# Stick-breaking layer: memory query projections ahead of the first pair, and the memory attention's steps dealt out from the first unit on

## The chip, the cores and the metric

One NeuronCore of one Trainium2 chip runs the whole program. The metric is device time in microseconds (us), the median of three timed executions. A profiled execution is one more, with its own time and a span from its first to its last instruction. Engines: PE is TensorE (its weight loads, PEld, overlap), DVE is VectorE, ACT is ScalarE, POOL is GpSimd, SP is SyncE.

## The reference

A trunk of two layers over 512 tokens of width 1024, all in float32. Layer 0 mixes with a gated delta rule, layer 1 with stick-breaking attention; both also attend over 256 memory tokens. The part that the change touches is layer 1's mixer:

```python
q, k, v = ...                          # 12 heads of 64
for blk in range(4):                   # blocks of 128 queries
    z = einsum('bthd,bshd->bhts', q[blk], k[:t1]) * 0.125
    log_1m_beta = where(before, log_sigmoid(-z), 0)
    tail = cumsum(log_1m_beta, reversed) - log_1m_beta
    a = where(before, exp(log_sigmoid(z) + tail), 0)
    out[blk] = a @ v
mem_q = proj[..., 3 * W:]              # 4 heads of 64
cross = softmax(mem_q @ mem_k.T * 0.125) @ mem_v
y = concat([mix, cross]) @ w_out       # then norm, residual and the MLP
```

## The kernel before

Every matrix product is done in three passes of a split format: each float32 operand is cut by ACT into a rounded high part (L199, `whi`) and by DVE into the rest (`split_lo`, L176, `wlo`), and PE adds hi*hi, hi*lo and lo*hi into one PSUM bank (`mm3`, L207 to L213; the matmuls are on L212). The activations live transposed, as `h_hi` and `h_lo`. PSUM has eight banks: four of the tag `acc` and four of the tag `g` (L89).

**Order of the work.** The Python text gives each instruction a place, and that is its rank. When the program is made, each engine's queue is filled by taking the ready instruction of the best rank, and an instruction whose tile has no free slot yet is passed by until one comes free. So an instruction of later rank runs early when its inputs and a slot are there, and on the chip each engine then runs its queue in order.

**The stick-breaking stage** (L1261 to L1301). `sb_values` (L1032) makes the six value tiles `vv`, one for each pair of heads, in a ring of six slots with the tag `v`. `sb_qk` (L1062) projects one pair: two pieces of 24 matmuls, each handed out in slices of 9, 9 and 6 (`fm_slices`, L220), each holding one `acc` bank from its first matmul until DVE has read it (L1071 to L1077). `stick_breaking` (L1148) then runs 36 units, three for each head, the two heads of a pair one step apart. Step n does three things:

- `sb_scores` of unit n: matmuls into a `g` bank, three ACT functions (L1100 to L1102), then DVE's max-and-add (L1103), a cast and a split.
- `sb_weights` of unit n-2: the cumulative sums as matmuls (L1122), ACT's exponential, a DVE cast (L1128) and a POOL subtraction (L1129) into two-slot tiles.
- `sb_av` of unit n-4: weights times values (L1141). A head's three units add up in one `acc` bank, which is held from the first of them until ACT and DVE have copied it (L1145, L1146). A pair's value tile is let go after its second head, which for pair p is step 6p+10.

After each step the loop of L1289 asks the next pair's projection for a slice, and asks the generator `fill` (L1284) for as many steps as `FILLN` (L1316) has for this n: one row of six numbers for each pair of heads.

`fill` hands out the memory work. `mem_queries` (L1279) is two projections like the ones above, six steps of 9, 9 and 6 matmuls, with the results put away by L664 (ACT) and L665 (DVE). `mem_attention` (L669) is 20 steps for four heads and two halves of the tokens:

- eight *scores* steps (4 matmuls L691; DVE max L694; two ACT exponentials L698; DVE reciprocal L700 and two multiplications L702), with two slots for the result `p`;
- eight *turn* steps (4 transposes L711 into an `acc` bank; then two ACT copies L714 and two DVE splits into the tiles `pT`), two `pT` tiles for each head. These tiles have the tag `v`: they take slots of the ring of value tiles;
- four *values* steps (4 matmuls L722, an ACT copy L725, a DVE addition L726), in an `acc` bank.

The order is scores 1, scores 2, turn 1, scores 3, turn 2, scores 4, turn 3, values 1, and so on to turn 8 and values 4.

In this kernel the 6 + 20 steps go out at every second n: the six query steps at n = 1 to 11, the first nine steps of the attention at n = 13 to 29, and its last eleven at n = 30 to 36.

**After the stage.** `out_early` (L787) multiplies the first three of eight row blocks of `w_out`, 36 matmuls into all four `acc` banks, and `out_proj` (L801) goes on; neither's first blocks need the memory result or the last pair.

Of the kernel before, what the change touches and what calls it, by code (L numbers as in the profile page):

```python
# [62 lines left out]
def drain(gen):  # L63
    for _ in gen:
        pass
# [1104 lines left out]
def build(ctx, tc, a, out):  # L1170
# [27 lines left out]
    with tc.tile_pool(name="gdn", bufs=1, reuse_waits="tile") as gp:  # L1198
# [11 lines left out]
        def alloc(name):  # L1210
            if name == "p":
                return gp.tile([P, 2, NMEM], F32, name=name, tag="t2", bufs=3)
            if name == "o":
                return gp.tile([P, S], F32, name=name, tag="t2", bufs=3)
            t = gp.tile([P, 2, S], F32R, name=name, tag="kq" if name == "pTh" else "UI", bufs=3)
            return t[:, 0], t[:, 1]

        def fill(gi):
            if gi < 2:
                yield from k.qkv_group(gi + 1, hi, lo, gp, parts[gi + 1],  # L1220
                                       k.gates((2 * gi, 2 * gi + 1), hi, lo, mixT))
            else:
                yield from k.gates((4, 5), hi, lo, mixT)
                for c in range(2):
                    qm.append([gp.tile([P, S], F32R, name="qm", tag=x, bufs=2) for x in ("kT", "vT")])
                    yield from k.mem_q(win[4 * H + 1 + c], hi, lo, qm[c])
                yield from k.mem_attention(0, qm, alloc, mixT)
                yield from k.out_early(0, mixT, st)
        st = {}
        for gi in range(3):  # L1230
            weave(k.gdn_group(gi, parts[gi], gp, mixT), fill(gi), SCALE[gi], lambda n: n % 3 or k.tick(1))
# [29 lines left out]
    with tc.tile_pool(name="sb", bufs=1, reuse_waits="tile") as sp:  # L1261
        tc.keep_in_program_order(nc.scalar.preload_act_table_set("natural_log_exp_and_others"))
        vv = k.sb_values(hi, lo, sp, later[0])
        mixT = k.act.tile([P, KC, S], F32, name="mixT", bufs=1)
        qks = [{} for _ in range(H)]
        drain(k.sb_qk(0, hi, lo, sp, qks[0]))
        qm = []

        def alloc(name):
            if name == "p":  # L1270
                return sp.tile([P, 2, NMEM], F32, name=name, bufs=2)
            if name == "o":
                return sp.tile([P, S], F32, name="sb_o", bufs=1)
            if name == "w":
                return sp.tile([P, 512], F32, name=name, tag="p", bufs=2)
            t = sp.tile([P, 2, S], F32R, name="pT", tag="v", bufs=H)
            return t[:, 0], t[:, 1]

        def mem_queries():  # L1279
            for c in range(2):  # L1280
                qm.append([sp.tile([P, S], F32R, name="qm", bufs=4) for x in "hl"])
                yield from k.mem_q(a["w_b_qk"][2 * H + c], hi, lo, qm[c])

        def fill():  # L1284
            yield from mem_queries()
            yield from k.mem_attention(1, qm, alloc, mixT)
        extra = fill()
        proj = None
        for n in k.stick_breaking(qks, vv, sp, mixT):  # L1289
            pair, u = divmod(n + LAG, 6)  # L1290
            if (u == 0 or n == 0) and pair + 1 < H:
                proj = k.sb_qk(pair + 1, hi, lo, sp, qks[pair + 1])
            if u < 5:
                next(proj, None)
            for _ in range(FILLN[min(n // 6, H - 1)][n % 6]):
                next(extra, None)
            if u == 5:
                drain(proj)
        drain(extra)
        st = {}  # L1300
        drain(k.out_early(1, mixT, st))  # L1301
# [11 lines left out]


GROUPS = (16, 12)
FILLN = ((0, 1, 0, 1, 0, 1),) * 5 + ((2, 1, 2, 1, 2, 1),)  # L1316
SCALE = (1.0, 1.0, 1.0)
YS = (2.0, 2.0, 1.5, 0.5, 2.0, 1.8, 1.2, 1.2, 1.2, 1.2, 0.8, 0.9, 0.8, 3.0)
_F = np.ascontiguousarray
# [49 lines left out]
```

## Time and profile before

| | us |
|---|---|
| median of 3 runs (1320.36 to 1321.84) | 1320.38 |
| the profiled execution | 1318.39 |
| its span | 1316.7 |
| PE busy in the span | 1275.9 (97%) |
| DVE busy | 861.8 (65%) |
| ACT busy | 717.5 (54%) |
| POOL busy | 163.9 (12%) |

The profiled execution has 1.69 us around its span and is 1.99 us under the median. Busy time of PE is counted from modelled ends of pipelined matmuls, so a PE shown as full need not be at its peak; the other engines' busy time is a fair measure. The granted clock of PE is 0.993 over the span.

### The profile page before, as it was taken

To read this page: it belongs to the slowest core of one execution; us is meant where nothing else is said; L and a number is where in the kernel's file an instruction comes from. 1 tells how busy PE (TensorE), PEld (TensorE's weight loads), DVE (VectorE), ACT (ScalarE), POOL (GpSimd) and SP (SyncE) were. 2 spreads that over 40 slices of the span, in tenths; PEclk is the share of its full clock that TensorE was granted. 3 is DMA by queue.
4 is the path that set the end of the run, shared out by engine and by line. 5 is a ranking of instruction groups with operands and counts; after the bars stand their busy time and mean duration, and the time that the engine had idled before them with its cause. 6 is when DMAs were issued, how large, how long until landed. Compare 5 with 4: busy or idle time off the path is not lost.

```text
span 1316.7 us, 18097 instructions
## 1 busy us (share of the span) xinstructions
PE 1275.9 (97%) x6620; PEld 1070.0 (81%) x6620; DVE 861.8 (65%) x1588; ACT 717.5 (54%) x1378; POOL 163.9 (12%) x196
## 2 busy tenths in 40 slices
PE   7999999998999999999999999998999999999997
PEld 7788878887788888878888988786788888878886
DVE  7677695877663264555788678999573255455776
ACT  8654435446455454444565567878455344454561
POOL 2511313010021000000000013223130000000000
PEclk9999999999999999999999999999999999999999
DMA  7551654415689878644454426222679944544441
GB/s 242 192 166 58 161 130 117 123 51 143 210 245 266 233 190 243 195 145 143 148 186 139 157 75 150 76 64 64 208 255 256 257 127 144 148 141 150 152 144 64
DMA packets 82153, 209.39 MB, mean 159 GB/s; under 512 B 6720, under 2 KB 11840, under 8 KB 81616
## 3 DMA queue, kind: packets, MB, share of 16 engines
q1 hardware_dynamic: 62192, 164.12, 37.7%
q0 software_dynamic: 19296, 43.06, 16.4%
q8 instruction: 52, 0.85, 0.3%
q10 hardware_dynamic: 576, 1.05, 0.2%
q14 instruction: 37, 0.30, 0.1%
HBM read 199.29 MB, written 67.63 MB: 203 GB/s over the span
## 4 chain that ended last, share of the span: by engine, by line
PE 80%; DVE 10%; ACT 6%; issue 2%; DMA 1%; POOL 0%; SPq 0%; DVEq 0%; POOLq 0%; ACTq 0%
PE ps_acc L212 45%; PE ps_g L955 21%; PE ps_g L212 4%; PE ps_g L526 1%; PE ps_g L1122 1%; DVE wlo L176 1%; PE ps_g L389 1%; PE ps_g L518 1%; ACT whi L199 1%; PE ps_g L488 1%; ACT scrap L281 1%; DVE cv L360 1%; PE ps_g L295 1%; DVE sb_e L1103 1%; PE ps_acc L1141 1%
## 5 line engine op out<-in xcount | busy, mean ns | idle before, releaser
L212 PE MATMUL ps_acc<-h_hi,whi 128*128 128x512 f32 (+1 forms) x888 | 338.1, 381 | 0.0
L212 PE MATMUL ps_acc<-h_hi,wlo 128*128 128x512 f32 (+1 forms) x888 | 337.5, 380 | 0.0
L212 PE MATMUL ps_acc<-h_lo,whi 128*128 128x512 f32 (+1 forms) x888 | 335.1, 377 | 0.0
L176 DVE TENSOR_TENSOR wlo<-raw,whi 128x1024 fp32r<-128x1024 f32 x134 | 169.2, 1264 | 141.3 <-ACT whi L199 133.9
L955 PE MATMUL ps_g<-whi,sh 128*128 128x512 f32 x784 | 261.1, 395 | 0.0
L199 ACT ACTIVATE whi<-raw 128x1024 fp32r<-128x1024 f32 x134 | 141.8, 1059 | 203.0 <-PE ps_g L955 94.1
L176 DVE TENSOR_TENSOR wlo<-xc,whi 128x1024 fp32r<-128x1024 f32 x89 | 108.8, 1224 | 151.2 <-ACT whi L199 149.0
L212 PEld LDWEIGHTS ps_acc<-h_hi,wlo 128*128 128x128 f32 x888 | 167.5, 189 | 34.0 <-DVE wlo L176 3.9
L212 PEld LDWEIGHTS ps_acc<-h_hi,whi 128*128 128x128 f32 x888 | 167.8, 189 | 28.8 <-ACT whi L199 1.6
L212 PEld LDWEIGHTS ps_acc<-h_lo,whi 128*128 128x128 f32 x888 | 167.9, 189 | 28.4
L955 PEld LDWEIGHTS ps_g<-whi,sh 128*128 128x128 f32 x784 | 147.6, 188 | 34.5
L199 ACT ACTIVATE whi<-xc 128x1024 fp32r<-128x1024 f32 x89 | 94.3, 1060 | 137.1 <-PE ps_g L955 92.5
L955 PE MATMUL ps_g<-wlo,sh 128*128 128x512 f32 x392 | 154.8, 395 | 0.0
L955 PEld LDWEIGHTS ps_g<-wlo,sh 128*128 128x128 f32 x392 | 73.9, 189 | 17.2
L882 POOL DMA_DIRECT2D sum<-w_down x56 | 51.5, 1332 | 181.8 <-DMA sum<-w_down 104.4
L176 DVE TENSOR_TENSOR sh<-ua,sh 128x512 fp32r<-128x512 f32 x98 | 66.7, 685 | 4.7 <-ACT sh L936 4.7
L1129 POOL TENSOR_TENSOR sb_al<-sb_a,sb_ah 128x384 fp32r<-128x384 f32 (+1 forms) x36 | 41.2, 1144 | 154.8 <-DVE sb_ah L1128 133.1
L936 ACT ACTIVATE sh<-ua 128x512 fp32r<-128x512 f32 x98 | 59.9, 618 | 0.3
L212 PE MATMUL ps_acc<-ua 128*128 128x512 f32 x224 | 57.3, 391 | 0.0
L978 POOL DMA_DIRECT2D ua<-park x4 | 2.3, 574 | 388.6 <-DVE sh L176 381.2
L212 PEld LDWEIGHTS ps_acc<-ua 128*128 128x128 f32 x224 | 42.0, 188 | 8.9
L212 PE MATMUL ps_acc<-whi,h_hi 128*128 128x256 f32 (+1 forms) x144 | 44.5, 326 | 0.0
(352 smaller groups left out, 2148.2 us busy)
## 6 DMA issues: line engine op xcount, KB each, us to landing
sum<-w_down POOLq DMA_DIRECT2D x56, 512.0 KB, 9.9
xc<-w_up SPq DMA_DIRECT2D x38, 512.0 KB, 3.9
xc<-w_down SPq DMA_DIRECT2D x30, 512.0 KB, 3.9
xc<-sum SPq DMA_DIRECT2D x29, 512.0 KB, 4.0
sum<-w_down SPq DMA_DIRECT2D x28, 512.0 KB, 6.5
sum<-sum SPq DMA_DIRECT2D x28, 512.0 KB, 5.4
raw<-w_in_a SPq DMA_DIRECT2D x27, 512.0 KB, 3.8
raw<-sum SPq DMA_DIRECT2D x27, 512.0 KB, 3.7
```

The lines of the kernel that those rows point to most:

```text
L176: self.nc.vector.tensor_tensor(out=lo, in0=src, in1=f(hi), op=ALU.subtract)
L199: self.nc.scalar.activation(out=hi, in_=raw, func=AF.Copy)
L212: self.nc.tensor.matmul(out, lhsT=l, rhs=r, start=start and k == 0 and i == 0, stop=stop and k == n - 1 and i == 2)
L281: nc.scalar.activation(out=self.scrap(m), in_=x[:, j * m:(j + 1) * m], func=AF.Square, accum_out=ssq[:, j:j + 1])
L295: op = nc.tensor.transpose(b[:, j, i * P:(i + 1) * P], xs[i][:, (kc + j) * P:(kc + j + 1) * P], self.ident)
L360: nc.vector.scalar_tensor_tensor(out=acc[:, j:], in0=b[:, :S - j], scalar=w[:, 3 - j:4 - j], in1=acc[:, j:], op0=ALU.mult, op1=ALU.add)
L389: self.nc.tensor.transpose(tp[:, t], src(t), self.ident)
L488: nc.tensor.matmul(sb[:, j], lhsT=self.sel[:, s4 + j], rhs=ud, start=True, stop=True)
L882: self.tc.keep_in_program_order(nc.gpsimd.dma_start(out=dst, in_=src, accum_op=ALU.add))
L936: nc.scalar.activation(out=s[:, 0], in_=src, func=AF.Copy)
L955: nc.tensor.matmul(y[t], lhsT=l, rhs=r, start=new and d == 0 and z == 0 and m == 0, stop=d == nd - 1 and z == 1 and m == 2, skip_group_che ...
L1129: nc.gpsimd.tensor_tensor(out=u["al"], in0=a, in1=f(u["ah"]), op=ALU.subtract)
```

## The change

The two query projections leave `fill` and are drained before it is made, that is after the first pair's projection and before unit 0. `fill` keeps the 20 steps of the attention alone, and `FILLN` is dealt anew: one step at n = 1, 3, ..., 23, two in each row's first half from n = 24 on, so that the 20th goes out at n = 35. No instruction is added or taken away.

```diff
         def fill():
-            yield from mem_queries()
             yield from k.mem_attention(1, qm, alloc, mixT)
+        drain(mem_queries())
         extra = fill()
...
-FILLN = ((0, 1, 0, 1, 0, 1),) * 5 + ((2, 1, 2, 1, 2, 1),)
+FILLN = ((0, 1, 0, 1, 0, 1),) * 4 + ((1, 1, 0, 1, 0, 1),) * 2
```

In the new numbering scores 1 to 4 stand at n = 1, 3, 7 and 11, turns 1 to 3 at n = 5, 9 and 13, values 1 at n = 15, and turns 7 and 8 and values 3 and 4 in the last six steps.

## Rows read from the trace of the kernel before

**Rows 1.** The page, busy time of each engine over the span.
```profile
PE 1275.9 (97%) x6620; PEld 1070.0 (81%) x6620; DVE 861.8 (65%) x1588; ACT 717.5 (54%) x1378; POOL 163.9 (12%) x196
```

**Rows 2.** Windows: stretch, length; busy (count) of PE, PEld, DVE, ACT, POOL; clock, DMA.
```profile
745.00:763.00 18.00, 18.00 (x110) 16.02 (x108) 7.31 (x12) 6.72 (x13) 0.00 (x0) 1.00 0.53 186
765.40:818.30 52.90, 52.90 (x288) 44.50 (x286) 43.56 (x70) 38.33 (x69) 13.02 (x13) 1.00 0.44 104
818.30:870.10 51.80, 48.89 (x282) 41.52 (x280) 48.54 (x84) 41.00 (x86) 13.38 (x13) 1.00 0.29 81
870.10:895.00 24.90, 23.63 (x135) 19.72 (x135) 23.90 (x42) 20.81 (x43) 8.29 (x8) 1.00 0.38 81
895.00:926.00 31.00, 26.58 (x144) 19.45 (x143) 29.70 (x66) 24.08 (x61) 12.55 (x11) 1.00 0.19 63
```

**Rows 3.** The chain that ended last: start, us, what.
```profile
765.95 4.09 PE ps_acc L212 x18
```

**Rows 4.** Groups by line, 763 to 926 us: count, busy us, mean ns, idle before.
```profile
L176 DVE TENSOR_TENSOR wlo<-raw,whi 128x1024 fp32r<-128x1024 f32 x13 | 15.8, 1216 | 3.0 <-ACT whi L199 2.9
L702 DVE TENSOR_SCALAR p<-p,sm 128x256 f32<-128x256 f32 x16 | 8.6, 576 | 0.1
L176 DVE TENSOR_TENSOR pT<-ps_acc,pT 128x256 fp32r<-128x256 f32 x16 | 6.6, 416 | 0.8 <-ACT pT L714 0.7
L694 DVE TENSOR_REDUCE nmx<-ps_acc 128x2 f32<-128x512 f32 x8 | 5.5, 684 | 0.1
L665 DVE SCALAR_TENSOR_TENSOR qm<-ps_acc,qm 64x512 fp32r<-64x512 f32 x4 | 2.8, 690 | 0.1
L726 DVE TENSOR_TENSOR mixT<-ps_acc,sb_o 64x512 f32<-64x512 f32 x4 | 2.7, 685 | 0.1
```

**Rows 5.** Windows of the maximum L694 alone: stretch, length, DVE busy (count), clock, DMA.
```profile
818.30:870.10 51.80, 2.04 (x3) 1.00 0.29 81
...
895.00:926.00 31.00, 2.75 (x4) 1.00 0.19 63
```

**Rows 6.** Windows of the tile pT alone; columns as in rows 2, without POOL.
```profile
818.30:870.10 51.80, 0.00 (x0) 0.00 (x0) 1.67 (x4) 1.54 (x4) 1.00 0.29 81
...
895.00:926.00 31.00, 3.88 (x12) 2.02 (x12) 4.13 (x10) 3.83 (x10) 1.00 0.19 63
```

**Rows 7.** Timeline: start, us, instruction; units 0 and 35, a query result, the last mixT.
```profile
762.60 0.22 PE L1092 MATMUL ps_g<-sbqh,sbkk 128*128 128x128 f32 x1
765.39 0.49 ACT L1100 ACTIVATE sb_e<-ps_g 128x384 f32<-128x384 f32 x1
821.12 0.59 ACT L664 ACTIVATE qm<-ps_acc 64x512 fp32r<-64x512 f32 x1 [0.66 <-DVE qm L665]
912.72 0.60 ACT L1100 ACTIVATE sb_e<-ps_g 128x512 f32<-128x512 f32 x1
927.13 0.69 DVE L1146 TENSOR_TENSOR mixT<-ps_acc,sb_o 64x512 f32<-64x512 f32 x1 [0.72 <-ACT sb_o L1145]
```

**Rows 8.** Timeline of who holds `acc` banks around turn 3 (876 to 904 us).
```profile
876.18 0.60 PE L711 MATMUL ps_acc<-ident,p 128*128 128x128 f32 x4
878.90 0.39 PE L212 MATMUL ps_acc<-h_hi,whi 128*128 128x512 f32 x1
882.38 0.30 PE L1141 MATMUL ps_acc<-sb_ah,v 128*128 128x128 f32 x1
886.40 0.40 PE L1141 MATMUL ps_acc<-sb_al,v 128*128 128x512 f32 x1
888.78 0.42 DVE L176 TENSOR_TENSOR pT<-ps_acc,pT 128x256 fp32r<-128x256 f32 x1
889.26 1.19 PE L722 MATMUL ps_acc<-pT,mv 128*128 128x512 f32 x4 [0.68 <-DVE pT L176]
894.42 0.69 DVE L176 TENSOR_TENSOR sbkk<-ps_acc,sbkk 64x512 fp32r<-64x512 f32 x1
903.35 0.66 DVE L1146 TENSOR_TENSOR mixT<-ps_acc,sb_o 64x512 f32<-64x512 f32 x1
```

## The prediction

> **What bounds the kernel now.** I read the page first, then windows over the stage that the change touches, then the chain of waits inside it, and last the groups of instructions and the timeline. The page says that PE is busy for 97% of the span and DVE for 65% [rows 1]. Over 1317 us that hides stages with other limits, so the windows come next. They are cut where the scores of units 0, 12, 24 and 30 reach ACT: 765.4, 818.3, 870.1 and 895 us, with 926 as the end of the stage.
>
> The reader is to see in them that the limit changes inside the stage [rows 2]. In the first twelve units PE is full (52.90 of 52.90 us) and DVE has 9.3 us left over (43.56 of 52.90). In the next twelve DVE is busy for 48.54 of 51.80 and PE, even by its generous count, for 48.89. From 895 us on DVE is busy for 29.70 of 31.00 and PE for 26.58. So the stage begins with PE as its bound and ends with DVE as its bound, and the chain of waits agrees: it starts out as runs of projection matmuls, 18 of them in 4.09 us [rows 3], and later goes through ACT and DVE. The counts tell why. The first stretch holds both query projections, which are much PE work and little DVE work. The last one holds four of the eight scores steps (the maximum, x4) [rows 5], five of the eight turns (two splits each, x10) and three of the four values steps (x12 matmuls) [rows 6].
>
> Ahead of the stage, from 745 to 763 us, PE is full too, with DVE busy for only 7.31 of 18 us [rows 2]. That is the neighbourhood into which the queries move.
>
> **The change part by part.** No instruction comes or goes. So I price the places: how much of DVE's and of PE's work each stretch holds afterwards, and how long the stretch must then last. For a stretch that DVE bounds I divide its DVE work by the share at which DVE ran in the three later stretches, (48.54 + 23.90 + 29.70) / (51.80 + 24.90 + 31.00) = 0.948 [rows 2]. The work of a step is the sum of its DVE durations [rows 4]: a scores step 0.684 + 2 x 0.576 = 1.84 us, a turn 2 x 0.416 = 0.83, a values step 0.69. A query projection has a weight split of 1.22 and two results of 0.69.
>
> *The queries ahead of unit 0.* 48 matmuls at 4.09 / 18 = 0.228 us [rows 3] are 10.9 us in which PE is full and no unit's scores are issued. Unit 0's first matmul moves from 762.60 [rows 7] to 773.5. Its ACT step does not move as far: today it stands at 765.39 [rows 7], 2.8 us behind that matmul, since ACT is still copying the second projection of the first pair. Afterwards that copying is long done, and I put it some 0.7 us behind the matmul, at 774.2, which is 8.8 late. The ends are 8.8 and 10.9; I take +9.0, near the first, since nothing else stands before it on ACT. Two more issues move with the steps: the two weight loads on SP's queue, which then stand ahead of pair 1's, and the two background copies that each finished projection lets out. DMA was at 0.53 there and 0.44 behind it [rows 2], so I price them at nothing; were a weight late, PE would wait in the open, at most for one piece (5.5 us).
>
> *Units 0 to 11.* PE loses 10.9 of its 52.9 us, so the bound is now DVE: 43.56, less two weight splits and two of the four results (the other two are late, at 821.12 [rows 7]), which is 3.81, plus four scores steps, 7.36. That is 47.1, or 49.7 at 0.948, against 52.9: -3.2.
>
> Only scores steps come in, not turns, and this is the point of the change that the ring decides. A head's two `pT` tiles take slots of the value tiles. Those of pairs 0 and 1 are let go at n = 10 and n = 16, so turns 1 and 2, which are dealt out at n = 5 and 9, can't be finished before n = 16, about where turn 1 stands today (n = 17).
>
> *Units 12 to 23.* Out go the two late query results (1.38), three scores and two turns (7.18). In come five turns, one values step and two scores steps (8.52). 48.54 becomes 48.5, or 51.2 us: -0.6.
>
> *Units 24 to 29.* One of each (3.36, what the neighbours leave of 8, 8 and 4) becomes two scores, one turn and one values step (5.20). 25.7 / 0.948 = 27.2 against 24.9: +2.3.
>
> *The last stretch.* Four scores, five turns and three values steps (13.6) become two turns and two values steps (3.0). If DVE stays the bound, 10.5 / 0.948 = 11.1 us go. But the last unit's own chain runs through every engine: it starts at 912.72 and its sum into `mixT` ends at 927.82 [rows 7]. If those 15.1 us stay as they are, only the 17.7 us before them shrink, by 10.5 / 29.7 of their length, 6.3. I take -9.0, the middle, because a chain with DVE free waits less but can't vanish. What is late next is that chain, and behind it `out_early`, which is PE work with no need of the last pair and can fill PE's free time once two of four banks are free.
>
> *Banks held by turns that can't finish.* The trace shows one such turn: turn 3's transposes at 876.18 take a bank, the slot for its low part comes free with the last matmul of pair 3 (886.40), DVE lets the bank go at 889.2, and PE then starts the values step that had stood still for 0.68 us [rows 8]. Afterwards turns 1 and 2 both stand so, from about n = 9 to 16. A head holds a bank for 21.6 us (882.38 to 904.01) and a projection for 16.2 (878.90 to 895.11) [rows 8]. A pair needs 2 x 21.6 + 2 x 16.2 = 75.6 bank-us, and on two banks this takes 37.8 us where twelve units in 51.8 give a pair 25.9. If nothing gives way, 7 units of hold cost 7/6 x 11.9 = 13.9 us. If a projection is squeezed to its 24 x 0.228 = 5.5 us of PE time, 54.2 on two banks is 27.1, and the cost is 1.4. I take +1.4, since it agrees with two holds at the 0.68 that one costs today, and since a unit's weights may lag two steps behind its scores.
>
> The sum is 9.0 - 3.2 - 0.6 + 2.3 - 9.0 + 1.4 = -0.1 us on a span of 1316.7. The profiled execution was 1318.39, 1.99 under the median of the runs shown, and I carry the difference over to that median: 1320.3 us. The change moves work from a full place to another nearly full place, and the start that it delays costs what the end gives back.
>
> A rule weighs against the change here. The rows show the first stretch with both kinds of work woven together, at full PE and 0.82 of DVE [rows 2]. The Trainium skill, in "Perfetto Trace Analysis", section "Optimization Strategy", says that where the most-contended engine changes over time, interleaving the regimes may help. Dealing out the attention follows it; draining the queries in one block undoes it. By the rule the block costs its whole 10.9 us instead of 9.0, and the sum would be +1.8.
>
> **The rivals.**
>
> *Bank famine, slower.* Between n = 9 and 16 the heads and projections get two of four `acc` banks; a head that waits for one keeps its two-slot weight tiles, the next units' weights stop behind them, and with four score tiles in flight DVE runs out of work. For it speaks that turn 3 shows the mechanism on one bank [rows 8]; against it that projections have been paced by rank, not by need. It decides as soon as turn 2's transposes get their bank before the second pair's first head gets its own. At the middle of its two ends, 7.5 in place of 1.4: +6.0, 1326.4 us.
>
> *DVE fills up, faster.* With scores steps at hand from the first unit, DVE may run at its full share and the end may give all 11.1: 47.1 - 52.9 + 48.5 - 51.8 + 25.7 - 24.9 - 11.1 + 8.8 = -10.6 without bank waits. Nothing in the trace runs at 1.0 over such a length, so I take somewhat over half: -6, 1314.4 us. For it speaks that DVE had 9.3 us free in the first stretch, against it that 0.948 held in all three later ones [rows 2].
>
> *The attention does not move.* The order is made by readiness, and the ring lets no turn go earlier. If the scores steps, too, wait for banks behind earlier ranks, only the queries move: the first stretch is then 39.8 of DVE (41.9) against 42.0 of PE, -10.9, the second -1.5, the start +9.0. That is -3.4, 1317.0 us.
>
> **How the numbers follow.** About 2.6 us (0.2%) is what a measurement of this kernel tells from no change. The forecast, -4 to +3 around -0.1, has 0.42, of which 0.09 lie past the bound on the fast side and 0.06 on the slow. Bank famine has 0.25, all slower; the full DVE 0.21, all faster; the attention that does not move 0.12, of which 0.07 are past the bound. So faster is 0.09 + 0.21 + 0.07 = 0.37, slower 0.06 + 0.25 = 0.31, no change 0.32. The forecast's own range is 1316.4 to 1323.3. The range to hold the time 8 times in 10 takes in both outer rivals' middles, 1313 to 1327, and leaves out the far half of bank famine's prices and of the full DVE's.
>
> **What would show it.** Right: unit 0's ACT step at about 774; units 12 and 30 about 6 and 8 us later than now; DVE near 0.95 from the first unit on; the last stretch shorter by 6 to 11. Turn 1's low part stands at or behind n = 16. Wrong: an idle DVE of several us between units 9 and 16 with a head's first matmul waiting for a bank (famine); a share of 0.97 or more throughout, and `out_early` done inside the last unit's chain (faster); scores steps no earlier in units than now.

## The result: slower by 0.9%

| | before | after |
|---|---|---|
| median, runs side by side | 1320.37 us (1319.66 to 1321.84, 4 runs) | 1331.28 us (1330.38 to 1331.81, 4 runs) |
| span of the profiled execution | 1316.7 us | 1328.7 us |
| granted clock over that span | 0.993 | 0.989 |

The ratio is 1.0093, with a 95% interval of 1.0071 to 1.0114. The forecast was 1320.3 us, with a range of 1313 to 1327.

The page of the kernel after shows no loss in its sums; this line answers to [rows 1]:

```profile
PE 1283.1 (97%) x6620; PEld 1075.9 (81%) x6620; DVE 857.6 (65%) x1588; ACT 717.0 (54%) x1378; POOL 165.3 (12%) x196
```

The loss is in the windows of the stage, cut where the scores of units 0, 12, 18, 24 and 30 reach ACT and where the last sum into `mixT` ends. They answer to [rows 2], with the columns named there: stretch, length, busy of PE, PEld, DVE, ACT, POOL, then the granted clock, the DMA share and GB/s.

```profile
776.30:821.90 45.60, 43.98 (x255) 37.24 (x253) 40.92 (x74) 37.87 (x80) 14.87 (x13) 1.00 0.51 123
821.90:855.00 33.10, 29.41 (x149) 23.89 (x148) 22.94 (x44) 19.83 (x42) 8.60 (x7) 0.90 0.19 55
855.00:886.60 31.60, 28.45 (x153) 23.82 (x152) 26.02 (x48) 22.61 (x50) 5.37 (x5) 0.95 0.11 34
886.60:912.30 25.70, 23.74 (x135) 19.48 (x134) 23.75 (x43) 20.35 (x42) 9.02 (x9) 1.00 0.32 69
912.30:940.00 27.70, 24.14 (x127) 18.22 (x126) 23.87 (x49) 20.79 (x46) 11.03 (x10) 1.00 0.35 111
```

Units 12 to 23 are the two middle rows of trouble: 33.1 + 31.6 = 64.7 us, where the kernel before takes 51.8. In the first of them DVE is busy for 22.94 of 33.10 us, a share of 0.69, and in the same row the clock is at 0.90. The stretches around them are shorter than before or nearly as long. Behind the stage nothing changes: from the last sum into `mixT` to the end of the span are 388.6 us, before 388.8.

Ahead of the stage the two profiles differ already. The last copy of the first pair's projection, which the change leaves alone, stands here in the kernel before and then in the changed one:

```profile
764.77 0.59 ACT L1073 ACTIVATE sbqh<-ps_acc 64x512 fp32r<-64x512 f32 x1
766.04 0.59 ACT L1073 ACTIVATE sbqh<-ps_acc 64x512 fp32r<-64x512 f32 x1
```

That is 1.27 us later, with a granted clock of 0.97 over the first 100 us where the kernel before has 0.98. So of the 12.0 us by which the span grew 1.3 are not the change's, and 10.7 are, which agrees with the medians (10.9).

Inside the bad stretch, smaller windows (same columns) show the order of events:

```profile
830.00:835.00 5.00, 3.97 (x28) 3.36 (x26) 4.97 (x8) 4.90 (x12) 0.00 (x0) 1.00 0.27 73
835.00:840.00 5.00, 3.57 (x22) 2.71 (x22) 3.35 (x11) 3.87 (x8) 2.99 (x2) 1.00 0.08 32
840.00:845.00 5.00, 4.14 (x18) 3.23 (x18) 4.96 (x11) 3.55 (x9) 1.00 (x1) 0.61 0.00 0
845.00:850.00 5.00, 5.00 (x19) 4.03 (x19) 1.32 (x4) 0.00 (x0) 0.56 (x1) 0.70 0.01 3
850.00:855.00 5.00, 5.00 (x30) 4.44 (x29) 2.12 (x2) 2.74 (x5) 1.74 (x2) 1.00 0.00 0
```

First PE runs short of work (7.54 us busy of 10 between 830 and 840), then its clock falls, and then, from 845 on, PE is full while DVE does 3.44 us of work in 10. The timelines say what happened; each line is a start, a duration and an instruction, with the idle time before it and what ended that. First PE, which holds the banks (some lines of 796 to 858 us):

```profile
796.53 0.60 PE L711 MATMUL ps_acc<-ident,p 128*128 128x128 f32 x4
...
818.26 0.66 PE L711 MATMUL ps_acc<-ident,p 128*128 128x128 f32 x4 [0.75 <-DVE mixT L1146]
...
829.56 0.40 PE L212 MATMUL ps_acc<-h_hi,wlo 128*128 128x512 f32 x1
...
834.94 0.33 PE L1141 MATMUL ps_acc<-sb_ah,v 128*128 128x128 f32 x1 [0.33 <-ACT p L698]
...
835.51 0.60 PE L711 MATMUL ps_acc<-ident,p 128*128 128x128 f32 x4
...
839.92 0.47 PE L1141 MATMUL ps_acc<-sb_al,v 128*128 128x512 f32 x1
...
844.69 0.78 PE L212 MATMUL ps_acc<-h_hi,whi 128*128 128x512 f32 x1
845.26 0.63 PE L212 MATMUL ps_acc<-h_lo,whi 128*128 128x512 f32 x1
845.69 0.63 PE L212 MATMUL ps_acc<-h_hi,wlo 128*128 128x512 f32 x1
...
848.36 0.23 PE L1141 MATMUL ps_acc<-sb_ah,v 128*128 128x128 f32 x1
```

Then ACT's copies of turns 1 and 2, two for each turn:

```profile
816.50 0.38 ACT L714 ACTIVATE pT<-ps_acc 128x256 fp32r<-128x256 f32 x1
...
818.96 0.39 ACT L714 ACTIVATE pT<-ps_acc 128x256 fp32r<-128x256 f32 x1
...
842.40 0.38 ACT L714 ACTIVATE pT<-ps_acc 128x256 fp32r<-128x256 f32 x1 [0.39 <-DVE pT L176]
...
843.10 0.37 ACT L714 ACTIVATE pT<-ps_acc 128x256 fp32r<-128x256 f32 x1
```

And DVE, with the splits that end both turns and what it waits for after them:

```profile
841.96 0.74 DVE L176 TENSOR_TENSOR pT<-ps_acc,pT 128x256 fp32r<-128x256 f32 x2
...
843.09 0.84 DVE L176 TENSOR_TENSOR pT<-ps_acc,pT 128x256 fp32r<-128x256 f32 x2
...
848.91 0.36 DVE L1128 CAST sb_ah<-sb_a 128x384 fp32r<-128x384 f32 x1 [2.85 <-PE ps_acc L1141]
852.69 0.43 DVE L1128 CAST sb_ah<-sb_a 128x512 fp32r<-128x512 f32 x1 [3.42 <-PE ps_acc L1141]
```

Turn 1's transposes take an `acc` bank at 796.5 and turn 2's take a second at 818.3. Their high parts find a slot of the ring at 816.5, their low parts only behind pair 1's last matmul, so both banks come free together at 843.5 to 843.9, after 47.0 and 25.7 us. Turn 3 takes a third bank at 835.5, and a head the fourth at 834.9. From then to 843.5 no bank is left. The holds also lengthen themselves: pair 1's second head, whose last matmul (839.92) frees the slots of the low parts, gets its own bank only at 834.9. The next pair's projection stops at 829.8 and goes on at 844.7, 14.9 us later; the next head begins at 848.4. When the banks come, PE first makes up the 24 late projection matmuls, with one head's four matmuls between them, and DVE's casts wait 2.85 and 3.42 us for the two-slot weight tiles that these matmuls (L1141) have yet to read. In the kernel before, turn 3 stood for 13.0 us with one bank and the values step waited 0.68 us for it [rows 8]. The mechanism is the same, with three turns in place of one.

### The profile page after: what moved, and what is told of

Same layout as the page of the kernel before. It is cut to its first block, busy times and chain, and to the rows that moved or that the text cites. A ratio compares the mean times of both kernels' runs of the same rounds, so it can differ in the third digit from the quotient of the medians.

```text
span 1328.7 us, 18094 instructions
## 1 busy us (share of the span) xinstructions
PE 1283.1 (97%) x6620; PEld 1075.9 (81%) x6620; DVE 857.6 (65%) x1588; ACT 717.0 (54%) x1378; POOL 165.3 (12%) x196
## 6 DMA issues: line engine op xcount, KB each, us to landing
sum<-w_down POOLq DMA_DIRECT2D x56, 512.0 KB, 10.2
```

## The experiments

Each ran beside the kernel before, on the same chip; gains and losses are ratios to it with their 95% intervals. The theory: turns dealt out before the ring has slots hold `acc` banks. The rivals: the block of queries ahead of unit 0 costs its PE time, or the dealing itself is bad.

**Queries alone.** The first nine attention steps go back to their old places; the queries stay ahead.

```diff
-FILLN = ((0, 1, 0, 1, 0, 1),) * 4 + ((1, 1, 0, 1, 0, 1),) * 2
+FILLN = ((0,) * 6,) * 2 + ((0, 1, 0, 1, 0, 1),) * 3 + ((2, 1, 2, 1, 2, 1),)
```

> The queries are drained ahead of unit 0 as in the changed kernel, but the 20 attention steps stand at the n of the kernel before (nine at n = 13 to 29, eleven at n = 30 to 36). Bank theory (the loss comes from turns dealt out before the ring has slots for them; they hold banks that heads and projections need): turns 1 and 2 stand behind n = 16, nothing holds a bank for more than 15 us, and the time is that of the third rival, about 1317 us (1315 to 1321). Start theory (the 10.9 us of queries ahead of unit 0 are the loss, since the units behind can't run faster): about 1331 us, unit 12 and all later ones late by about 11 us.

Measured: 1318.92 us, ratio 0.9999 (0.9984 to 1.0014). Unit 0 starts at 777.2, 11.8 us late; of these 2.2 us were there at the last copy L1073 (766.94, before 764.77), so the block delays it by 9.7. The first twelve units give 10.2 back. Their window, with the columns above:

```profile
777.20:819.90 42.70, 42.70 (x240) 35.89 (x239) 39.76 (x63) 35.29 (x67) 13.09 (x13) 1.00 0.55 131
```

The block is paid and given back, so the queries are not the loss. This is also the rival "the attention does not move": priced at -3.4 us, it measures none.

**Late turns.** Two scores steps early, all turns only when their slots are free.

```diff
+FILLN = ((0,) * 6, (0, 1, 0, 0, 0, 1), (0, 0, 0, 0, 0, 1), (1,) * 6, (1,) * 6, (1, 1, 1, 1, 1, 0))
```

> Queries ahead; scores 1 and 2 at n = 7 and 11, turn 1 at n = 17, the other 17 steps one at each n from 18 to 34. Bank theory: turn 1 finds both its slots free, the famine is gone and the last pair is lighter than before: 1312 to 1320 us. Start theory: about 1330 us, as the queries stand where they stand in the changed kernel.

Measured: 1320.63 us, ratio 1.0011 (0.9993 to 1.0029). No turn stands in its trace as in the changed kernel, and no loss can be told; nor did the gain come that the range of 1312 to 1320 us allowed for.

**Other slots.** The changed dealing, step for step, but heads 1 and 3 put their `pT` tiles into the ring of the weights (`whi`, `wlo`).

```diff
+        turns = []
...
-            t = sp.tile([P, 2, S], F32R, name="pT", tag="v", bufs=H)
+            turns.append(name)
+            if (len(turns) - 1) // 2 % 2 == 0:
+                t = k.wp.tile([P, 2, S], F32R, name="pTw", tag="whi" if name == "pTh" else "wlo", bufs=NW)
+            else:
+                t = sp.tile([P, 2, S], F32R, name="pT", tag="v", bufs=H)
```

> The changed kernel with the same numbers of steps at each n, but the pT tiles of heads 0 and 2 take a slot each of the weights' split rings (whi, wlo; three of four slots are left to the weights), so that turns 1 and 2 never wait for a value tile. Bank theory: banks are let go within some 5 us, turn 1 stands near n = 5, DVE has no gap of several us before unit 18, and the time comes to 1314 to 1322 us; if the weights' rings get tight, up to 4 us more. Start theory: 1329 to 1332 us, no matter which slots the turns take.

Measured: 1321.39 us, ratio 1.0017 (0.9999 to 1.0035). Turn 1's copies now run behind its transposes, at 797.95 and 800.25 (the tile is named `pTw` here), not at 816 and 842:

```profile
797.95 0.38 ACT L714 ACTIVATE pTw<-ps_acc 128x256 fp32r<-128x256 f32 x1 [1.01 <-PE ps_acc L711]
800.25 0.39 ACT L714 ACTIVATE pTw<-ps_acc 128x256 fp32r<-128x256 f32 x1 [0.97 <-DVE pTw L176]
```

Units 12 to 17 take 25.7 us instead of 33.1, with DVE busy for 24.87:

```profile
824.40:850.10 25.70, 24.44 (x136) 20.32 (x137) 24.87 (x44) 20.41 (x42) 6.64 (x6) 1.00 0.28 88
```

The dealing without the standing turns loses at most 0.35%. This is the run that separates the theory from "the dealing itself".

**One hold, two holds.** Only turn 1 early; then turns 1 and 2 early, turn 3 late.

```diff
+FILLN = ((0, 1, 0, 1, 0, 1), (0,) * 6, (0, 0, 0, 0, 0, 1), (1,) * 6, (1,) * 6, (1, 1, 1, 0, 1, 0))
...
+FILLN = ((0, 1, 0, 1, 0, 1), (0, 1, 0, 1, 0, 0), (0, 0, 0, 0, 0, 1), (1,) * 6, (1,) * 6, (1, 0, 1, 0, 0, 0))
```

> Queries ahead; scores 1, scores 2 and turn 1 at n = 1, 3 and 5, then nothing until n = 17, and one step at nearly every n from there. Turn 1 alone holds one bank from about n = 4 to 16 (some 45 us); turn 2 comes only when its slots are there. Bank theory with a threshold: with three banks left the heads (21.6 us) and projections (16.2 us) need 75.6 bank-us for each pair and have 77.7 in 25.9 us, so one hold costs little: 1313 to 1322 us. Bank theory without a threshold (each held bank costs alike): about half the loss, 1324 to 1328 us. Start theory: about 1330 us.

> The changed kernel with turns 1 and 2 where it has them (n = 5 and 9) and turn 3 and all that follows from n = 18 on, when their slots are free. So two acc banks are held at once (about 818 to 844 us), and never a third. If two of four banks are enough for the famine, as the prediction reckoned, the loss is 5 to 11 us against the kernel before, with DVE's share in units 12 to 17 under 0.8. If it takes the third hold (turn 3 from 835 us), the loss is 0 to 2 us, with DVE above 0.9 in that stretch. I expect about +6.

Measured with one hold: 1318.66 us, ratio 0.9992 (0.9978 to 1.0007). With two: 1323.98 us, 1.0034 (1.0017 to 1.0051), that is +4.5 us. Units 12 to 17, one hold and then two:

```profile
822.10:845.10 23.00, 23.00 (x134) 19.62 (x133) 22.21 (x36) 18.83 (x36) 6.65 (x6) 1.00 0.29 82
```

```profile
822.50:850.10 27.60, 25.52 (x139) 21.06 (x138) 22.77 (x43) 19.49 (x38) 6.81 (x7) 1.00 0.23 66
```

One of four banks held for 42.4 us (798.2 to 840.6) costs nothing that can be told, although the low part of turn 1 stands nearly as long as in the changed kernel. So one copy that waits is not what hurts. Two banks held together (818.9 to 844.3) cost 4.5 us (2.2 to 6.7), just under the 5 to 11 that were expected. DVE's share is 0.97 with one and 0.825 with two, where "under 0.8" was expected.

**Turn 2 in another bank.** The changed kernel, with turn 2's transposes in a bank of the tag `g`.

```diff
-            b = self.bank("acc").rearrange("p (m t) -> p m t", m=2)
+            b = self.bank("g" if i == 1 and (h, t2) in ((0, 2),) else "acc").rearrange("p (m t) -> p m t", m=2)
```

> The changed kernel with nothing moved, but turn 2 puts its transposes into a bank of the tag g instead of acc. Its copies still wait for the same slots, and so do turns 1 and 3. If what hurts is the number of acc banks held at once, one fewer takes away most of the loss: 0 to 4 us against the kernel before. If it is the waiting copies themselves (their place in the queues of ACT and DVE) or the order of the steps, the loss stays at 9 to 12 us. If scores are short of a g bank instead, the loss stays too, but the idle time stands in front of L1092 and not of L1141 or L212.

Measured: 1323.24 us, ratio 1.0032 (1.0012 to 1.0051). No step moved in the program and no slot came sooner; turn 2 still stands (its copies run at 818.4 and 845.0). Of the changed kernel's loss some 8 us are gone with one `acc` bank given back, and with them the fall of the clock (1.00 from 830 to 865). Two `acc` banks are still held together, by turn 1 and from 833.6 on by turn 3, and what is left, +4.2, is about the price of two holds. That the scarce thing is the bank, and neither the slot nor the order, is shown by this run.

**More matmuls.** The changed kernel with three further matmuls ahead of the scores of units 13 to 18, overwritten at once; and, as a control, the kernel before with the same.

```diff
+        for _ in range(more):
+            nc.tensor.matmul(zb, lhsT=kk[:, :P], rhs=qh, start=True, stop=True, skip_group_check=True)
...
-                self.sb_scores(units[n], pool)
+                self.sb_scores(units[n], pool, 3 if 13 <= n < 19 else 0)
```

> The changed kernel as it is, with three more matmuls of 512 columns ahead of the scores matmuls of each of units 13 to 18, into the same g bank, overwritten by the scores: 18 x 0.228 = 4.1 us more of PE work where PE stands idle in the changed kernel (3.3 us of 15 between 830 and 845). They hold no bank and release nothing sooner. If the granted clock that fell to half at 841.1 and 858.2 us (10.2 us in all, up to 5.1 us of work) is a part of the loss of its own, it no longer falls there and the loss shrinks from 11 to 6 to 8 us. If the loss is the banks alone, or if the clock falls for another reason, it stays at 11 to 15.

> The control to e11_more_matmuls: the kernel before with the same 18 matmuls in units 13 to 18. There the granted clock doesn't fall in the stage, so they can only cost: 0 us where DVE binds, at most 4.1 where PE does. I expect +1 to +3.

Measured: 1327.22 us, ratio 1.0052 (1.0035 to 1.0070); the control 1320.23 us, 1.0006 (0.9991 to 1.0021). PE is busy for 13.37 of the 15 us between 830 and 845, where the changed kernel has 11.68, and the clock stays whole:

```profile
830.00:845.00 15.00, 13.37 (x78) 10.42 (x77) 11.99 (x26) 12.71 (x28) 4.34 (x4) 1.00 0.13 35
855.00:865.00 10.00, 9.41 (x50) 7.41 (x49) 9.44 (x21) 7.93 (x19) 3.31 (x3) 1.00 0.10 40
```

The changed kernel's own windows of the same stretches have 0.87 and 0.83:

```profile
830.00:845.00 15.00, 11.68 (x65) 9.30 (x64) 13.29 (x28) 12.31 (x27) 4.00 (x3) 0.87 0.12 35
855.00:865.00 10.00, 7.63 (x33) 5.75 (x32) 8.82 (x16) 7.57 (x16) 1.01 (x1) 0.83 0.17 53
```

With more work on PE the program became faster, by 3 us (medians less their own references) to 5 us (ratios). No bank came free sooner: the splits that end turns 1 and 2 are over at 845.2 us here, at 843.9 in the changed kernel. The profiles agree: from unit 0's ACT step to the last sum are 163.7 us without these matmuls and 159.9 with them. So the loss has two parts, banks of about 7 us (the matmuls' own cost in it) and 3 to 5 of a clock that falls behind PE's idle time. With two holds, where PE is busy for 13.30 of the same 15 us, it does not fall (1.00 in both stretches).

The time between runs also holds what the clock does elsewhere in the program. A length inside each profile, from the copy L1073 shown above to the end of the last sum, leaves that out: 163.1 us in the kernel before and 174.0 in the changed one, 162.2 with the queries alone, 163.3 with one hold, 166.6 with two, 165.9 with turn 2 in another bank, 170.2 with more matmuls and 165.2 in their control. Against the kernel before these are +10.9, -0.8, +0.2, +3.5, +2.8, +7.2 and +2.2. That is nearly the order of the medians. The control says that the matmuls may cost 2 us of their own, so three holds at a whole clock stand at 5 to 7 us.

**Attempts at a faster version.** `e7_spread_both` spreads all 26 steps evenly, one query projection between the first attention steps, with the other slots of `e3_other_slots`. Three more take the attention's scores steps out of the `acc` banks.

```diff
+            yield from mem_query(0)
+            other, steps = mem_query(1), k.mem_attention(1, qm, alloc, mixT)
+            for s in steps:
+                yield s
+                for r in other:
+                    yield r
+                    break
...
+FILLN = ((0, 1, 0, 1, 0, 1), (1, 0, 1, 1, 0, 1), (1, 0, 1, 1, 0, 1), (1, 1, 1, 0, 1, 1), (1, 1, 1, 0, 1, 1), (1, 1, 1, 1, 1, 0))
...
-            b = self.bank("acc").rearrange("p (t m) -> p t m", t=2)
+            b = self.bank("g" if i else "acc").rearrange("p (t m) -> p t m", t=2)
```

> A version meant to be better than both: the first query projection in units 1 to 5 as in the kernel before, the second dealt out between the first attention steps (heads 3 and 4 alone need it), the 26 steps spread 3, 4, 4, 5, 5, 5 over the six rows, and the slots of heads 1 and 3 as in e3_other_slots. No start is delayed (unit 0 at 765.4 us) and no turn holds a bank. If DVE then runs near 0.948 from unit 6 on, the stage's 146.8 us of DVE work take some 157 us instead of 162.4: -5 us, with -2 to -7 as its ends. If the last unit's own chain or PE sets the end, 0 to -2.

> The kernel before, with one thing changed: the eight scores steps of the memory attention take a bank of the tag g instead of acc. In the kernel before, holds of acc banks, added up from the trace, come to 3.6 to 3.8 of 4 from unit 12 on, those of g banks to 3.1; the scores steps hold 44 bank-us of acc. If acc banks bind the stage even without any turn that stands, 44 bank-us at 3.75 banks are up to 11 us, of which I expect some: -2 to -6 us. If DVE alone binds from unit 12 on (the prediction's reading), it is 0 within 2.6 us; if the units are then short of g banks, it is slower by 2 to 5.

> The version e2_late_turns (queries ahead, turns only where their slots are free), with the scores steps in g banks as in e8_before_scores_g. Beside e2_late_turns (+1.3 us, span 1315.8): if acc banks bind, 2 to 6 us faster than the kernel before; if not, no change within 2.6 us.

> The version e7_spread_both with the scores steps in g banks. e7_spread_both lost 7.9 us with no turn standing; its middle stretches hold acc banks at 3.6 to 3.75 of 4 and DVE is at 0.85 to 0.90. If it lost for want of acc banks, the loss shrinks to 0 to 4 us; if it lost for another reason (slots of the weight ring, the order of the steps on PE), it stays at 6 to 9.

Measured: the spread 1327.44 us, ratio 1.0060 (1.0040 to 1.0080); the kernel before with scores in `g` banks 1319.34, 1.0001 (0.9984 to 1.0018); the late turns with it 1322.27, 1.0024 (1.0006 to 1.0043); the spread with it 1323.88, 1.0037 (1.0021 to 1.0052). The expectation of -5 us for the even spread failed, and so did the -2 to -6 us expected of the scores in `g` banks. The even spread's units 24 to 29 take 30.1 us against 24.9 [rows 2], and PE stands idle in them:

```profile
875.40:905.50 30.10, 25.20 (x149) 20.91 (x147) 27.12 (x48) 23.67 (x50) 8.14 (x8) 1.00 0.41 93
```

The clock has a part in it: in the profile of the even spread it is 0.94 in units 18 to 23 and 0.89 from 905.5 to 936 us, though no turn stands. With the scores steps in `g` banks the spread is some 3 to 4 us faster, but the intervals of the two overlap, and its clock falls in one stretch (0.90 in units 24 to 29) instead of two. So it is not shown that `acc` banks bind the spread; they don't bind the kernel before (1.0001). What else makes the even spread slower was not found. No version beats the kernel before.

## Why the prediction was wrong

**The step that failed is the last term, "banks held by turns that can't finish".** It stood at +1.4 with ends of 1.4 and 13.9. The two stretches that it acts on, units 12 to 23, take 64.7 us where the other terms gave 51.2: 13.5 more, near the far end. Not all of this is banks: with the clock kept whole by more matmuls the same units take 60.9 us, 9.7 more, the matmuls' own cost included. The mechanism was named, with two of the three turns and with their banks, and as a rival (bank famine) it got a chance of 0.25 and a middle price, +6.0; its size was off. Three things in its working show why.

- The low end let a projection be "squeezed to its 24 x 0.228 = 5.5 us of PE time", at a cost of 1.4 us. It did give way, and that is the cost: 24 matmuls pushed together at 844.7 stand in front of heads whose weights DVE needs, and DVE waits 6.3 us for them.
- Two holds were counted. Turn 3 is a third, from 835.5 on, and with a head in the fourth bank none is left for 8 us. Two holds cost +4.5 in the experiment; with three the loss was 12.3 by the ratio, and +6.9 with the clock kept whole.
- The price of one hold, 0.68 us, was carried to two as twice that. The experiments read -1.1 (-2.9 to +0.9), +4.5 (2.2 to 6.7) and, at a whole clock, +6.9 us (4.6 to 9.2) for one, two and three: the cost starts at the second bank. What the third costs at a whole clock is not clear of the noise.

To this comes what no term had: the granted clock falls at 841 and 858 us, behind PE's idle time, worth 3 to 5 us.

**The other terms.** The measured column is from the profiles of both kernels.

| term | predicted | measured |
|---|---|---|
| ahead of the change's place | 0 | +1.3 |
| start of unit 0 | +9.0 (8.8 to 10.9) | +9.7 |
| units 0 to 11 | -3.2 | -7.3 |
| units 12 to 23, holds included | +0.8 | +12.9 |
| units 24 to 29 | +2.3 | +0.8 |
| last stretch | -9.0 (-6.3 to -11.1) | -5.1 |
| behind the stage | 0 | -0.2 |
| sum, on the span | -0.1 | +12.1 |

The span itself grew by 12.0; the rest is rounding.

*The start* was nearly right. Unit 0's ACT step stands 10.95 us later than before, of which 1.27 were there ahead of the change. Its first matmul, at 774.74, is 1.2 us later than predicted, and that is this lag: 48 matmuls at 0.228 us were the right price. The rest is the ACT step, 1.6 us behind that matmul, where 0.7 was taken. "Nothing else stands before it on ACT" was wrong: ACT cuts a weight and puts the last query results away just then. The timeline of ACT around unit 0's step (L1100) answers to [rows 7]:

```profile
774.76 1.06 ACT L199 ACTIVATE whi<-raw 128x1024 fp32r<-128x1024 f32 x1 [1.78 <-PE ps_acc L212]
775.84 0.59 ACT L664 ACTIVATE qm<-ps_acc 64x512 fp32r<-64x512 f32 x1
776.34 0.47 ACT L1100 ACTIVATE sb_e<-ps_g 128x384 f32<-128x384 f32 x1
```

The prediction also weighed a rule of the Trainium skill, "Perfetto Trace Analysis", section "Optimization Strategy": interleaving regimes with different bounds may improve the time. By it the prediction put this term at 10.9; the trace has 9.7, nearer the 9.0 that was taken. The runs do not bear the rule out here: the queries drained in a block cost nothing in all (ratio 0.9999), and the two versions that interleave most, the change and the even spread, are the slowest.

*Units 0 to 11* gained twice what was predicted. Three scores steps come in, not four (the fourth, at 831, waited for a bank), so DVE's work is 40.92 us and not 47.1. At DVE's share of 0.90 that is 45.6 us. By an estimate half of this gain is work put off: the fourth scores step (1.84 us as priced) and the last results of one projection (8 operations L1075 in these units, before 10; 2.05 us). The scores steps were also cheaper than priced: their multiplications L702 take 0.35 us each in these units, where the mean of 0.576 was carried over. *The last stretch* lost less than its near end: the holds pushed the later steps back, so that DVE still has 23.87 us of work there, where 29.7 - 10.5 = 19.2 was reckoned, and the last unit's own chain, 15.1 us before, takes 12.3 from 927.73 on. The maxima (L694) of the stretches, 3, 1, 2, 1 and 1, and the turns' splits show this, as [rows 5, 6] do for the kernel before; the windows of tile `pT` (columns without POOL) for the last three stretches are:

```profile
855.00:886.60 31.60, 1.68 (x4) 0.84 (x4) 1.68 (x4) 1.80 (x5) 0.95 0.11 34
886.60:912.30 25.70, 1.20 (x4) 0.67 (x4) 1.67 (x4) 1.27 (x4) 1.00 0.32 69
912.30:940.00 27.70, 2.82 (x8) 1.35 (x8) 1.64 (x4) 1.54 (x4) 1.00 0.35 111
```

**The signs named ahead** pointed the right way. For "an idle DVE of several us between units 9 and 16 with a head's first matmul waiting for a bank" the prediction said famine. DVE's long idle time, 846 to 853 us, came between the scores of units 17 (841.5) and 18 (855.0), a little later than said, because it follows the release of the banks and not the hold. "The point from which it decides", turn 2's bank ahead of the second pair's first head, was one head early: that head got its bank at 811.4, before turn 2 (818.3), and the pair's second head waited until 834.9.

## What to carry to other kernels

A step that takes a bank before the slot for its result is free holds the one while it waits for the other. Before dealing such steps out earlier, set the hold of each (from its first matmul to the release of its slot) against the number of banks: here one of four was free of charge, a second cost some 4 us, and with a third, and the clock that fell behind it, the loss was 11 to 12. Work that "gives way" comes back in one block, and the price of that block is whoever waits behind it, not its own time. And a difference of a few us is best read inside the profiles, between an instruction ahead of the change and one behind it: here that took 1.3 us off a start that looked 10.95 us late.

## What the runs showed of the hardware

The granted clock fell to its lower level (1.2 GHz instead of 2.4) inside a program whose PE is 97% busy. In the 10 us before, 830 to 840, PE was busy for 7.54 us, and its longest wait there was 1.35 us. The late projection matmuls start 0.43 us apart at 845 us, against 0.228 [rows 3]. The Trainium skill says in "Perfetto Trace Analysis", section "Matmul Optimizations", that the matmul engine scales its power with use, so that matmuls should run back to back in batches; the trace agrees, and 18 useless matmuls (4.1 us of PE's time) kept the clock up and gave back some 3 to 5 us.

The clock also goes with most of the spread of one and the same kernel. In 91 executions of the kernel before, beside the experiments, the mean granted clock lay between 0.990 and 0.999 and the time between 1323.5 and 1314.0 us, with a correlation of -0.88; a clock lower by 0.001 goes with 0.9 us. It can differ far from any change: the profile of `e8_before_scores_g` has a span of 1312.6 us at 0.999, and where the profiles of the kernel before and of the changed one both have 0.74 it shows

```profile
287.00:300.00 13.00, 10.61 (x87) 9.78 (x86) 11.81 (x33) 9.84 (x29) 4.19 (x6) 1.00 0.65 125
```

though the program has the same instructions there. So a difference of a few us between two single profiles of such a kernel says nothing before their clocks are compared stretch by stretch.
